# Twelve chained transformer stages on one core: the order of issue is planned with turns on the shared SBUF ports and with other durations for a few operations

## Chip, core and metric

The kernel runs on one core of a Trainium2 chip. The metric is the device time of one execution in microseconds (us). Engines are named as in the profile: PE (TensorE matmul), PEld (TensorE weight load), DVE (VectorE), ACT (ScalarE), POOL (GpSimd), SP (SyncE, which issues the DMAs).

## What is computed

One sequence of 512 tokens with 1024 features passes through two blocks of two layers each, in fp32. The first block has, per layer, a mixer of three parts (a chunked mLSTM, a chunked HGRN2 and a sliding window attention), an MLP with squared ReLU, and a gated embedding:

```
for l in range(2):
    h = rms_norm(x, in_norm_g[l]);  y = h @ w_in[l] + b_in[l]
    x = x + concat([mlstm(y), hgrn2(y), swa(y)]) @ w_out[l]
    x = x + square(relu(rms_norm(x, mlp_norm_g[l]) @ w_up[l])) @ w_down[l]
    x = x + sigmoid(rms_norm(x, ple_norm_g[l]) @ w_ple_gate[l]) * rms_norm(p[l] @ w_ple_proj[l], ...)
```

The second block has, per layer, self attention over all 512 tokens (layer 0 dilated, layer 1 differential), cross attention to 256 memory rows and a SwiGLU MLP, each followed by a normed residual addition.

## The kernel before

**Stages.** The program is a list of twelve stages, `b10, mlp0, ple0, b11, mlp1, ple1, attn0, cross0, ffn0, attn1, cross1, ffn1`. Activations lie feature-major: `x` is eight tiles of 128 features by 512 tokens. Every weight is streamed from HBM as a raw tile (`wr`, three buffers, 512 KB each in most cases). ACT rounds it to a high part (`wh`), DVE subtracts to get a low part (`wl = wr - wh`), and a product is three matmuls: high by high, low by high, high by low. Activations are split in the same way (`hi` on ACT, `lo` on DVE). The function `wload` does the first, `split` the second.

**Work outside the large products.** `hgrn_att` (four calls, two in each of b10 and b11) forms for nine level lengths a tile `X` (DVE subtracts, ACT takes the exponential, POOL multiplies by `key`) and a tile `B` (two POOL multiplies), then multiplies `X` by `B` on PE and selects the results into a tile `d` with six `copy_predicated` for each block of 128 columns. `hgrn_gates` holds the scans (`tensor_tensor_scan`, output `G`). `rope` is a DVE multiply, a DVE `stream_shuffle` and two POOL operations. `k_stacks` splits `kl` between DVE and POOL. `swa` and `score` take a row maximum together with the mask in one `tensor_tensor_reduce` (in the trace CUSTOM_DVE_ANT_0). The softmax scaling `P<-P,s` is in part a POOL multiply whose second operand is a column broadcast along the row. `stat_add` adds squares on POOL (`acc<-acc,sq`).

**What sets the order.** No instruction is issued as written. A `Recorder` collects every operation with its dependences (`add`), gives it a duration and a latency (`cost`, from line 409) and a mark `lock` if it needs the SBUF ports that DVE and POOL share (`locks`, from line 393: on POOL everything but `memset`, on DVE operations with two SBUF inputs, and `tensor_copy` and `tensor_scalar` from SBUF to SBUF). `schedule` (from line 467) then plays the program through in time, one list of ready operations for each engine, lowest priority number first. It models the ports as one lock: `lock` is the engine that holds it and when it ends. `emit` (line 644) issues the operations in the order that this plan found. The chip runs each engine's list in that order, whatever the planned times were; semaphores hold the dependences. So durations and port rules in the planner change nothing but the order, the buffers that go with it, and which engine does an operation that is marked `either` (the residual additions `x<-x,u` and `x<-x,y`, lines 1476 and 1586).

In the kernel before, an operation that finds the lock held by the other engine is taken off its list and comes back when the lock ends:

```python
if o.lock and lock[0] != e and lock[1] > now + 1e-9:
    seq += 1
    heapq.heappush(events, (lock[1], seq, e, ("ready", o)))
    continue
```

At that moment both engines are served in the fixed order tensor, vector, scalar, gpsimd, sync. A DVE operation that is ready and needs the lock therefore takes it ahead of a POOL operation that has been waiting, as often as DVE has another one.

In the trace nearly all instructions carry one line, L654, since `emit` issues them all. Groups are told apart by their tiles' names.

Of the kernel before, what the change touches and what calls it, by code (L numbers as in the profile page):

```python
# [283 lines left out]
DVE_FIX, DVE_EL, PTR_V = 67.0, 1.042, 61.0  # L284
# [13 lines left out]
class Recorder:  # L298
# [110 lines left out]
    def cost(self, o, outs, ins):  # L409
        n = int(np.prod(o.args[0].shape[1:])) if isinstance(o.args[0], View) else 512  # L410
        psum = any(v.tile.pool.space is not None for v in ins + outs)
        if o.eng == "tensor":
            k = (1 if o.fn != "transpose" and o.args[1].dtype == F32R and n >= 256 else 2 if o.fn == "transpose" else 4)
            o.cols = k * n * o.args[1].shape[0] / 128.0
            if o.fn == "transpose":
                return max(50.0, n / 1.2 + 1), 200.0
            if o.args[1].dtype == F32R:
                return (n / 2.4 + 13.3 if n >= 256 else 4 * n / 2.4 + 3), 200.0
            m = o.args[0].shape[0]
            least = 278.0 if m > 64 and n < 32 else 210.0 if m > 64 else 104.0 if m > 32 else 49.0  # L420
            d = max(least, 4 * (n / 2.4 + 1))
            if o.args[0].shape[0] == 64:
                o.cols /= 2
                o.half, o.work = outs[0].box()[0] // 64, d
            return d, 200.0
        ptr = sum(1 for v in list(o.args[2:]) + [v for k, v in o.kw.items() if k != "accum_out"]
                  if isinstance(v, View) and len(v.shape) == 2 and v.shape[-1] == 1)
        if o.eng == "scalar":
            acc = 93.0 if "accum_out" in o.kw else 0.0
            return (51.0 if (ins or outs)[0].tile.pool.space is not None else 93.0) + n * ACT_EL + PTR_A * ptr + acc, 130.0  # L430
        if o.eng == "vector":
            if o.fn == "reciprocal":
                return DVE_FIX + 8 * n, 130.0
            if o.fn in ("tensor_reduce",):
                n = int(np.prod((ins or outs)[0].shape[1:]))
            if o.fn == "tensor_tensor_reduce":
                return DVE_FIX + n * DVE_EL + 80, 130.0
            el = DVE_EL
            if o.fn in ("tensor_copy", "tensor_scalar") and not psum:
                el /= 2  # L440
            return DVE_FIX + n * el + (PTR_V * ptr if o.fn in ("tensor_scalar", "scalar_tensor_tensor") else 0), 130.0
        if o.eng == "gpsimd":
            if o.kw.get("op") == ALU.pow:
                return 300 + 165 * n, 150.0
            if o.fn == "memset":
                return 88.0, 150.0
            return 100 + 2.2 * n, 150.0
        rows = o.args[0].shape[0] if isinstance(o.args[0], View) else 128
        return 60.0 + rows * n * 4 / 330.0, 2000.0

# [16 lines left out]
    def schedule(self, window=6000):  # L467
# [24 lines left out]
        ready = {e: [] for e in ("tensor", "vector", "scalar", "gpsimd", "sync")}  # L492
# [7 lines left out]
        events = []  # L500
# [14 lines left out]
            return True  # L515

        nd = 0
        lock = None, 0.0
        table, self.loads = None, 0
        while nd < N:  # L520
            if not events:
# [21 lines left out]
            for e in ready:  # L543
                if free_at[e] > now + 1e-9:
                    continue
                q = ready[e]
                skipped = []
                pick = late = None
                while q:
                    pr, i = heapq.heappop(q)  # L550
                    o = ops[i]
                    if done[i]:
                        continue
                    if i > oldest + window:
                        skipped.append((pr, i))
                        if len(skipped) > SKIP:
                            break
                        continue
                    if not can(o) or (o.mate and not can(o.mate)):
                        skipped.append((pr, i))  # L560
                        if len(skipped) > SKIP:
                            break
                        continue
                    if e == "scalar" and now - o.ready < PATIENCE and o.table and table not in o.table:
                        skipped.append((pr, i))
                        late = late or o
                        continue
                    if e == "gpsimd" and o.alt:
                        wait = max(0.0, free_at["vector"] - now)
                        wait += sum(ops[n].dur for x, n in ready["vector"] if x < pr and not done[n])  # L570
                        if wait + o.dur <= o.alt[0]:
                            skipped.append((pr, i))
                            continue
                    at = max([t.held[1] + TURN for t in o.banks if t.held[0] != e], default=0.0)
                    if at > now + 1e-9:
                        seq += 1
                        heapq.heappush(events, (at, seq, e, ("ready", o)))
                        continue
                    if o.lock and lock[0] != e and lock[1] > now + 1e-9:
                        seq += 1  # L580
                        heapq.heappush(events, (lock[1], seq, e, ("ready", o)))
                        continue
                    pick = o
                    break
                if pick is None and late is not None:
                    pick = late
                    skipped.remove((late.prio, late.idx))
                for it in skipped:
                    heapq.heappush(q, it)
                if pick is None:  # L590
                    continue
                commit = [pick]
                if pick.mate is not None:
                    commit.append(pick.mate)
                if e == "gpsimd" and pick.alt:
                    pick.eng, (pick.dur, pick.lat) = "gpsimd", pick.alt
                for o in commit:
                    for t in o.tiles:
                        if not t.alloc:
                            t.alloc = True  # L600
                            k = (t.pool.name, t.tag)
                            used[k] += 1
                            if t.first > oldest:
                                prof[k][oldest:t.first] += 1
                    if e == "scalar" and o.table and table not in o.table:
                        table = o.table[0]
                        o.dur += TABLE_LOAD
                        self.loads += 1
                    if e == "tensor":
                        o.dur = self.clocked(now, o)  # L610
                    o.start, o.end = now, now + o.dur
                    if o.lock:
                        lock = e, o.end
                    for t in o.banks:
                        t.held = e, max(o.end, t.held[1])
                    order.append(o)
                    done[o.idx] = True
                    nd += 1
                while oldest < N and done[oldest]:
                    oldest += 1  # L620
                if len(commit) == 2:
                    o.start += PAIR
                    o.end += PAIR
                free_at[e] = o.end
                seq += 1
                heapq.heappush(events, (o.end, seq, e, None))
                for o in commit:
                    seq += 1
                    fin = o.end + (o.lat if e == "sync" else RELEASE)
                    heapq.heappush(events, (fin, seq, e, ("free", o)))  # L630
                    for u in o.users:
                        u.nleft -= 1
                        lat = SAME[e] if u.eng == e and e != "sync" and not u.alt else o.lat + (TO_PE if u.eng == "tensor" else 0.0)
                        u.ready = max(u.ready, o.end + lat)
                        m = u.mate
                        if u.nleft == 0 and (m is None or m.nleft == 0):
                            seq += 1
                            at = u.ready if m is None else max(u.ready, m.ready)
                            heapq.heappush(events, (max(at, now), seq, u.eng, ("ready", u)))
# [1325 lines left out]
```

## Time and profile before

| | |
|---|---|
| median of 3 runs (lowest to highest) | 3153.84 us (3153.36 to 3154.46) |
| profiled execution, own time | 3149.14 us |
| its span, first to last instruction | 3147.4 us |
| PE busy | 2988.2 us (95%) |
| DVE busy | 1888.0 us (60%) |
| ACT busy | 1421.3 us (45%) |
| POOL busy | 767.7 us (24%) |
| mean granted TensorE clock | 0.975 of full speed |

A row of a group gives the count, the busy time, the mean length of one instruction, and the idle time of its engine just before it with what ended that. A row of the timeline gives start, length, engine, operation, tiles written and read, and the count; the idle time before it stands in brackets. An instruction that waits for the shared ports shows as a longer instruction, not as idle time. DVE instructions that follow each other overlap by some 0.08 us in the records.

### The profile page before, as it was taken

How to read it: one execution, taken by the hardware profiler on the slowest of the kernel's cores; microseconds unless marked ns; L12 is line 12 of the kernel's file. 1: busy time of each engine (PE TensorE's matmuls, PEld its weight loads, DVE VectorE, ACT ScalarE, POOL GpSimd, SP SyncE). 2: the span in 40 equal slices, each digit the busy share in tenths (PEclk: the TensorE clock that was granted, in tenths of full speed). 3: DMA queues.
4: the chain of work that ended last, by engine and by line, in shares of the span. 5: the costliest groups of instructions: out<-in, count | busy, mean ns of one | idle time of the engine just before them, and what ended most of it. 6: DMA issues, size and time to landing. Idle time of an engine off the chain costs nothing. (4 is left out here: it accounts for less than half of the span.)

```text
span 3147.4 us, 42909 instructions
## 1 busy us (share of the span) xinstructions
PE 2988.2 (95%) x16480; PEld 2465.0 (78%) x16480; DVE 1888.0 (60%) x3429; ACT 1421.3 (45%) x2611; POOL 767.7 (24%) x619
## 2 busy tenths in 40 slices
PE   8879999999888999999999899999999998999998
PEld 6647888887656788888777787888897777998887
DVE  7667544458668644457767665433489876663434
ACT  7456433346365522244666544322356555542222
POOL 2554100031645200024544303000055532120001
PEclk9989999999889999999999999999999999999999
DMA  3201323222220322222112322232331213232323
GB/s 133 71 22 49 113 94 101 94 94 70 78 61 26 116 99 96 97 98 90 52 54 61 118 78 94 94 100 94 99 120 41 71 59 96 92 117 94 100 93 103
DMA packets 86613, 269.97 MB, mean 86 GB/s; under 512 B 9608, under 2 KB 12680, under 8 KB 86408
## 3 DMA queue, kind: packets, MB, share of 16 engines
q1 hardware_dynamic: 86408, 267.22, 26.4%
q8 instruction: 130, 2.13, 0.3%
q14 instruction: 75, 0.61, 0.1%
HBM read 265.09 MB, written 2.10 MB: 85 GB/s over the span
## 5 line engine op out<-in xcount | busy, mean ns | idle before, releaser
L654 ACT CAST wh<-wr 128x1024 fp32r<-128x1024 f32 (+2 forms) x482 | 483.2, 1006 | 1148.4 <-PE s L654 398.6
L654 DVE TENSOR_TENSOR wl<-wr,wh 128x1024 fp32r<-128x1024 f32 (+2 forms) x482 | 602.2, 1254 | 279.8 <-ACT wh L654 278.3
L654 PE MATMUL g<-hi,wh 128*128 128x512 f32 (+1 forms) x1756 | 679.0, 387 | 16.9 <-ACT hi L654 11.8
L654 PE MATMUL g<-hi,wl 128*128 128x512 f32 (+1 forms) x1756 | 676.6, 385 | 2.4 <-DVE wl L654 2.4
L654 PE MATMUL g<-lo,wh 128*128 128x512 f32 (+1 forms) x1756 | 677.6, 386 | 0.6 <-DVE lo L654 0.6
L654 PE MATMUL s<-lo,wh 128*128 128x512 f32 (+1 forms) x1732 | 652.7, 377 | 4.6 <-DVE lo L654 4.6
L654 PE MATMUL s<-hi,wh 128*128 128x512 f32 (+1 forms) x1732 | 652.7, 377 | 4.4 <-ACT hi L654 4.2
L654 PE MATMUL s<-hi,wl 128*128 128x512 f32 (+1 forms) x1732 | 652.3, 377 | 0.0
L654 PEld LDWEIGHTS g<-hi,wh 128*128 128x128 f32 x1756 | 334.6, 191 | 79.3 <-ACT hi L654 12.9
L654 PEld LDWEIGHTS g<-hi,wl 128*128 128x128 f32 x1756 | 334.7, 191 | 61.7 <-DVE wl L654 3.0
L654 PEld LDWEIGHTS g<-lo,wh 128*128 128x128 f32 x1756 | 334.2, 190 | 61.0 <-DVE lo L654 1.5
L654 POOL TENSOR_TENSOR acc<-acc,sq 128x512 f32<-128x512 f32 x101 | 156.4, 1549 | 915.4 <-ACT sq L654 902.7
L654 PEld LDWEIGHTS s<-lo,wh 128*128 128x128 f32 x1732 | 326.4, 189 | 65.1 <-DVE lo L654 7.9
L654 PEld LDWEIGHTS s<-hi,wh 128*128 128x128 f32 x1732 | 326.5, 188 | 63.6 <-ACT hi L654 5.9
L654 PEld LDWEIGHTS s<-hi,wl 128*128 128x128 f32 x1732 | 326.4, 189 | 57.2 <-issue 0.3
L654 POOL TENSOR_TENSOR sq<-sq,sq 128x512 f32<-128x512 f32 x24 | 38.0, 1585 | 741.8 <-ACT sq L654 741.5
L654 POOL TENSOR_TENSOR P<-P,s 128x512 f32<-128x512 f32 x96 | 111.3, 1168 | 145.0 <-DVE s L654 115.4
L654 POOL TENSOR_TENSOR s<-s,mhalf 128x4 f32<-128x4 f32 (+2 forms) x53 | 72.3, 1363 | 189.9 <-DVE s L654 189.5
L654 PE MATMUL t<-const,P 128*128 128x128 f32 x560 | 98.0, 283 | 13.4 <-ACT T L654 2.8
L654 DVE SCALAR_TENSOR_TENSOR lo<-x,cols,hi 128x512 fp32r<-128x512 f32 (+1 forms) x112 | 102.2, 934 | 5.2 <-ACT hi L654 5.0
L654 PEld LDWEIGHTS t<-const,P 128*128 128x128 f32 x560 | 64.7, 142 | 45.7 <-issue 25.9
L654 ACT ACTIVATE hi<-x,cols 128x512 fp32r<-128x512 f32 (+1 forms) x112 | 73.3, 658 | 59.1 <-DVE x L654 53.4
(308 smaller groups left out, 4497.9 us busy)
## 6 DMA issues: line engine op xcount, KB each, us to landing
wr<-in_w_down_dram SPq DMA_DIRECT2D x96, 512.0 KB, 3.3
wr<-in_gu_dram SPq DMA_DIRECT2D x88, 512.0 KB, 3.3
wr<-in_w_up_dram SPq DMA_DIRECT2D x64, 512.0 KB, 3.3
wr<-in_w_in_fm_dram SPq DMA_DIRECT2D x34, 512.0 KB, 3.4
wr<-in_qk_dram SPq DMA_DIRECT2D x32, 512.0 KB, 3.3
wr<-in_xo_dram SPq DMA_DIRECT2D x24, 512.0 KB, 3.4
wr<-in_w_down_dram SPq DMA_DIRECT2D x32, 384.0 KB, 3.1
wr<-in_w_out_dram SPq DMA_DIRECT2D x32, 256.0 KB, 2.7
```

What stands on the lines that cost most here:

```text
L654: getattr(getattr(nc, o.eng), o.fn)(*[res(a) for a in o.args], **{k: res(v) for k, v in o.kw.items()})
```

## The change

The planner is changed in two places; no operation is added or removed. In `cost`, a scan is given 45 + 2.09 ns an element, `copy_predicated` a fixed 213 ns, `stream_shuffle` 30 ns more than before, `tensor_tensor_reduce` loses 80 ns, and a POOL operation with a broadcast operand has 1.75 instead of 2.2 ns an element. In `schedule`, the engine that finds the lock held is noted in `claim`; its operation stays on the list. When the lock ends, an engine that is not the claimant passes over its lock operations until 15 ns after that, and takes another operation from its list or waits. A claim ends when the claimant issues anything.

```diff
-            if o.fn == "tensor_tensor_reduce":
-                return DVE_FIX + n * DVE_EL + 80, 130.0
+            if o.fn == "tensor_tensor_scan":
+                return 45.0 + 2.09 * n, 130.0
+            if o.fn == "copy_predicated":
+                return 213.0, 130.0
+            if o.fn == "stream_shuffle":
+                return DVE_FIX + n * DVE_EL + 30, 130.0
...
-            return 100 + 2.2 * n, 150.0
+            return 100 + (1.75 if any(0 in v.arr.strides for v in o.args if isinstance(v, View)) else 2.2) * n, 150.0
...
-        lock = None, 0.0
+        lock, claim = (None, 0.0), None
...
-                    if o.lock and lock[0] != e and lock[1] > now + 1e-9:
-                        seq += 1
-                        heapq.heappush(events, (lock[1], seq, e, ("ready", o)))
-                        continue
+                    if o.lock:
+                        if lock[1] > now + 1e-9:
+                            if lock[0] != e:
+                                claim = claim or e
+                                again = lock[1]
+                                skipped.append((pr, i))
+                                continue
+                        elif claim not in (None, e) and now < lock[1] + 15.0:
+                            again = lock[1] + 16.0
+                            skipped.append((pr, i))
+                            continue
...
                 if pick is None:
+                    if again is not None:
+                        seq += 1
+                        heapq.heappush(events, (again, seq, e, None))
                     continue
+                if claim == e or now > lock[1] + 15.0:
+                    claim = None
```

## Rows read from the trace of the kernel before

**Rows 1.** The page: span, and busy time of each engine.
```profile
span 3147.4 us, 42909 instructions
PE 2988.2 (95%) x16480; PEld 2465.0 (78%) x16480; DVE 1888.0 (60%) x3429; ACT 1421.3 (45%) x2611; POOL 767.7 (24%) x619
```

**Rows 2.** Windows of b10, b11, attn0, attn1: length; PE, PEld, DVE, ACT, POOL; clock; DMA.
```profile
0.00:310.00 310.00, 260.68 (x1715) 198.21 (x1716) 212.43 (x541) 175.31 (x411) 137.66 (x147) 0.90 0.21 66
...
755.00:1055.00 300.00, 253.21 (x1562) 189.30 (x1560) 230.41 (x539) 170.05 (x408) 143.97 (x124) 0.90 0.20 64
...
1470.00:1790.00 320.00, 304.54 (x1816) 242.47 (x1813) 225.02 (x480) 192.90 (x367) 150.85 (x105) 0.99 0.22 69
...
2290.00:2640.00 350.00, 322.94 (x2061) 275.90 (x2060) 294.11 (x614) 201.51 (x419) 174.99 (x124) 0.98 0.23 74
```

**Rows 3.** Groups of PE whose idle time POOL ended.
```profile
L654 PE MATMUL s<-B,X 128*64 128x64 f32 (+2 forms) x448 | 44.0, 296 | 31.8 <-POOL B L654 20.0 <-DVE d L654 5.3 <-ACT A L654 3.9
...
L654 PE MATMUL s<-qs,kl 128*128 128x256 f32 (+2 forms) x32 | 10.0, 366 | 10.3 <-POOL kl L654 10.3
```

**Rows 4.** Timeline of DVE and POOL at 315 us.
```profile
315.17 1.23 DVE L654 TENSOR_TENSOR wl<-wr,wh 128x1024 fp32r<-128x1024 f32 x1
316.31 1.78 DVE L654 SCALAR_TENSOR_TENSOR lo<-x,cols,hi 128x512 fp32r<-128x512 f32 x1
...
315.81 3.44 POOL L654 TENSOR_TENSOR acc<-acc,sq 128x512 f32<-128x512 f32 x2 [1.82 <-ACT sq L654]
```

**Rows 5.** Timeline of DVE and POOL at 788 us.
```profile
788.42 3.37 DVE L654 TENSOR_TENSOR wl<-wr,wh 128x1024 fp32r<-128x1024 f32 x3
...
787.97 5.12 POOL L654 TENSOR_TENSOR B<-X,qh 128x256 f32<-128x256 f32 x2 [0.94 <-DVE cr L654]
...
800.23 3.00 POOL L654 TENSOR_TENSOR B<-X,qh 128x256 f32<-128x256 f32 x4
```

**Rows 6.** Groups of DVE by shape that read two SBUF tensors: count, busy, mean.
```profile
L654 DVE TENSOR_TENSOR wl<-wr,wh 128x1024 fp32r<-128x1024 f32 x406 | 531.8, 1314 | 258.7 <-ACT wh L654 257.6
L654 DVE SCALAR_TENSOR_TENSOR lo<-x,cols,hi 128x512 fp32r<-128x512 f32 x80 | 80.6, 1029 | 4.8 <-ACT hi L654 4.6
...
L654 DVE TENSOR_TENSOR qs<-z,qs 64x512 fp32r<-64x512 f32 x48 | 43.9, 915 | 9.2 <-ACT qs L654 7.9
...
L654 DVE TENSOR_TENSOR kl<-z,kh 64x512 fp32r<-64x512 f32 x36 | 37.0, 1028 | 22.6 <-ACT kh L654 21.2 <-PE t L654 1.0
```

**Rows 7.** Single tiles: least/median/longest ns, first to last start.
```profile
L654 DVE TENSOR_TENSOR wl<-wr,wh x482: 667/1224/2353, 5.2 to 3127.4; 128x1024 fp32r<-128x1024 f32 x137, 128x512 fp32r<-128x512 f32 x10, 128x768 fp32r<-128x768 f32 x10, 128x972 fp32r<-128x972 f32 x2
...
L654 DVE SCALAR_TENSOR_TENSOR lo<-x,cols,hi x112: 468/746/1800, 9.2 to 2785.0; 128x512 fp32r<-128x512 f32 x80, 128x256 fp32r<-128x256 f32 x32
...
L654 DVE TENSOR_TENSOR qs<-z,qs x48: 684/687/1719, 234.1 to 2539.2; 64x512 fp32r<-64x512 f32 x48
...
L654 DVE TENSOR_TENSOR kl<-z,kh x36: 665/691/1780, 191.5 to 2544.1; 64x512 fp32r<-64x512 f32 x36
```

**Rows 8.** Operations whose planned duration changes: tiles, groups and a timeline row.
```profile
L654 POOL TENSOR_TENSOR P<-P,s x96: 1035/1042/1877, 257.3 to 2558.2; 128x512 f32<-128x512 f32 x96
...
L654 DVE TENSOR_TENSOR_SCAN G<-ls,zero 128x64 f32<-128x64 f32 x16 | 3.1, 268 | 0.0
...
L654 DVE COPY_PREDICATED d<-hm,s 128x64 f32<-128x64 int32 x96 | 23.0, 248 | 6.9 <-PE s L654 4.5
...
149.97 1.67 DVE L654 COPY_PREDICATED d<-hm,s 128x64 f32<-128x64 int32 x6 [1.46 <-PE s L654]
...
97.51 0.95 DVE L654 COPY_PREDICATED d<-hm,s 128x64 f32<-128x64 int32 x6
```

**Rows 9.** Timeline of DVE and POOL at 1501 us.
```profile
1501.33 0.19 DVE L654 TENSOR_SCALAR s<-s 128x1 f32<-128x1 f32 x2
...
1500.02 2.04 POOL L654 TENSOR_TENSOR P<-P,s 128x512 f32<-128x512 f32 x2 [0.99 <-DVE s L654]
```

**Rows 10.** Groups of DVE: small scalings of one column.
```profile
L654 DVE TENSOR_SCALAR s<-s 128x1 f32<-128x1 f32 x161 | 20.9, 143 | 0.3
```

More of the change, by code (lines that the diff above doesn't have):

```diff
@@ L547, in schedule @@
                 skipped = []
-                pick = late = None
+                pick = late = again = None
                 while q:
```

## The prediction

> **What bounds the kernel now.** I read the page first. PE is busy for 2988.2 of 3147.4 us [rows 1], so all that an order of issue can win lies in the 159.2 us in which PE is idle, and in what a low clock costs beside them. Next come the windows, cut at the stages [rows 2]. PE is idle for 310 - 260.7 = 49.3 us in b10, 300 - 253.2 = 46.8 in b11, 320 - 304.5 = 15.5 in attn0 and 350 - 322.9 = 27.1 in attn1: 138.7 us in 1280 us of span. The other eight stages share 20.5 us and can't be improved by an order. In these four DVE is busy for 69%, 77%, 70% and 84% of the time and POOL for 44% to 50%. These are the stages in which both engines are at work together, so they are where the ports matter. The clock was 0.90 of full speed in b10 and b11.
>
> Then I ask what ended PE's idle time. POOL ended 20.0 us of it ahead of the products of `X` and `B`, and 10.3 us ahead of the one that needs `kl` [rows 3]: 30.3 us, all in b10 and b11. DVE and ACT ended the rest in many small pieces.
>
> Last comes the ports' own price. An instruction that waits for them is longer in the trace. The mean against the median of the same operation gives the excess: `wl` (1314 - 1224) ns x 406 = 36.5 us, `lo<-x` (1029 - 746) x 80 = 22.6, `qs` (915 - 687) x 48 = 10.9, `kl` (1028 - 691) x 36 = 12.1 [rows 6, 7]. That is 82 us in which DVE stood still for POOL, and I found no other group of this size.
>
> **Does the chip take turns?** At 315 us it does [rows 4]. POOL asks at 315.81, while DVE's `wl` runs until 316.40. The next DVE instruction, a `lo`, starts at 316.31 and takes 1.78 us instead of 0.746: POOL went first, though DVE had its next instruction ready. The planner of before would have given DVE the ports again. So its plan holds POOL back too long and lets DVE run too smoothly, and the new plan is nearer to this row. At 788 us the chip does not take turns: two POOL multiplies take 5.12 us where four take 3.00 at 800 us, that is 3.6 us more, and meanwhile three `wl` pass in 3.37 us, undelayed [rows 5]. I take rows 4 as the common case: the medians of `qs` and `kl` are within 30 ns of their least values, and the longest are 1.03 and 1.1 us above them [rows 7], about one POOL operation (1.04 us in the median [rows 8]), which is what a DVE instruction pays that has lost one turn.
>
> **The change, part by part.**
>
> *The claim.* It adds no instruction and no wait on the chip; it moves instructions within the lists of DVE and POOL, and with them those of PE, ACT and SP (whose order of loads follows the weight buffers). It can win in two places. First, DVE. Where the plan now expects POOL to have its turn, it puts a DVE operation that needs no shared port (a move out of PSUM, for one) into that time, instead of a lock operation that on the chip would block the list behind it. What DVE loses, 82 us, reaches PE only where PE has nothing else: PE is idle for 138.7 / 1280 = 10.8% of these stages. Spread evenly, 82 x 0.108 = 8.9 us of it falls on PE. From both sides: nothing is won if no free operation is ready at those moments, all 8.9 if one always is. I take half, 4.5 us, since DVE is busy for some three quarters of the time and often has one. Second, POOL. The 30.3 us behind POOL are not removed, because POOL already gets its turns on the chip; what changes is that consumers are placed sooner after it, and its inputs ahead of other DVE work. Bounds: a loss of 10 us (one more stall like the one of `kl`) and a gain of 10 (one less). I take 5 us won, half of one such stall. Where a stall goes, the next thing late is DVE's `d` (5.3 us) and ACT's copies (3.9 us) on the same groups [rows 3], which is why I don't take more.
>
> *Scans.* The 64-column scan is recorded at 268 ns, and records overlap by some 80, so it holds DVE for about 188; the plan had 134, and has 179 now [rows 8]. The program has 66 scans; by the old and the new formula they gain 45 ns (64 columns) to some 500 ns (512 columns) each, all early in b10 and b11: about 7 us that the plan had not counted. On the chip nothing is shorter; I put the value at 0, between -2 and +2.
>
> *copy_predicated.* This one goes the wrong way. Six in a row take 1.67 us when each follows the last (289 ns a step) and 0.95 us when two chains interleave (about 145) [rows 8]. The plan had 134 plus 127 for the dependence, 261 a step, and now has 213 + 127 = 340. For 96 of them it believes that DVE is busy for 96 x 79 ns = 7.6 us more than before, in the stretches where `d` holds up PE. Worth 0, with -1 to +4 us: a slower plan of `d` puts PE's work behind it later.
>
> *Shuffle, mask and maximum, POOL with a broadcast.* 30 ns on 42 shuffles and 80 ns off 130 reductions move at most 1.3 and 10.4 us of planned DVE time, in stages where PE covers it. The POOL multiply is recorded at 1042 ns in the median; the plan had 1226 and has 996 [rows 8]. 96 of them, 22 us of planned POOL time, become available to the plan in swa, attn0 and attn1, which the chip had given already. All together 0, between -2 and +2.
>
> **The sum.** 4.5 + 5 = 9.5 us. The profiled execution took 3149.14 us, its span 3147.4 and 1.7 around it; it lies 4.7 us below the median of 3153.84. Its own time would become 3139.6, and the median 3153.8 - 9.5 = 3144.3, rounded to 3144.
>
> **Rivals.** *No difference.* The ports are given as in rows 5 often enough, or PE's idle time is set by chains (scan, exponential, multiply, product, select) that no order shortens. For it speaks that eight of twelve stages are PE work alone, and that POOL's turns come on the chip whatever the plan says. The time is 3153.8, give or take 6. The Trainium skill, in "SBUF — State Buffer", section "Who interferes with whom", says that whoever issues first has the shared pair for its whole instruction and the other blocks fully; it knows of no turn for the one who waits. By that rule the claim would describe nothing and this rival would hold; the 1.78 us of rows 4 speak against it, the 5.12 us of rows 5 for it.
>
> *Slower.* The planner marks the small column scalings `s<-s` as lock operations (161 of them). On the chip they don't wait: two take 0.19 us at 1501.33, in the midst of a POOL pair that runs from 1500.02 to 1502.06 [rows 9], and the mean over all is 143 ns [rows 10]. They stand between the row maximum and ACT's exponential in `score`, `cross` and `attn`. With a claim the plan passes over them at the end of a lock, waits for POOL's turn (1.04 us), and lets DVE take a longer operation of lower priority first (0.7 us, as `qs`). On the chip that is 0.7 us in front of a chain that PE waits for. It costs nothing where PE has other work; it decides if more than one in ten is moved onto a stretch where PE is idle: 16 x 0.7 = 11 us, so 3153.8 + 11 = 3165. DVE's 84% in attn1 makes that the place. Against it: these scalings come in bursts with other small ones, and priority brings them back at once.
>
> *The change hardly binds.* Any operation that the claimant issues ends its claim, so DVE's claims end at its next free operation. POOL has nothing but lock operations beside `memset`, so its claims hold; this rival is a part of the first.
>
> **How the numbers follow.** About 0.2%, 6.3 us, is what a measurement of this kernel can tell from no change. Forecast (a gain of more than that): 0.46. No difference: 0.30. Slower: 0.24. The forecast's own range is 3130 to 3147: both gains at their upper bounds give 8.9 + 10 = 19 us, and 2 to 5 more if the clock of 0.90 rises with less idle time. Reaching over the other cases, the range is 3128 to 3165, which leaves out a slower case beyond the price of one move in ten, and a gain beyond all bounds.
>
> **What would show it.** Right: PE's idle time falls by some 10 us in b10, b11 and attn1 together while PE's busy time stays; the means of `wl`, `lo` and `qs` fall towards their medians; POOL's share of PE's idle time falls below 25 us. Wrong on DVE: the excess of 82 us stays. Wrong on POOL: the waits for `B` or `kl` grow or new ones stand in their place. The slower rival: ACT's waits for `s` grow in attn1. The claim itself would be wrong if rows like 5 were found more often than rows like 4.

## The result, and the profile after

The changed kernel takes 3103.86 us (median of 4 runs, 3099.72 to 3105.31); the kernel before takes 3154.15 beside it. The ratio is 0.9838 with a 95% interval of 0.9821 to 0.9855: 50 us less, five times the forecast and outside its range. The profiled executions stand at 3105.31 and 3149.14 us, so the traces differ by 43.8 us, and what follows explains these. The other 6.5 us come from which execution was profiled: that of the kernel before is one of its faster ones, that of the changed kernel the slowest of its four.

The page of the changed kernel, span and busy time of each engine:

```profile
span 3103.5 us, 42865 instructions
PE 2983.3 (96%) x16480; PEld 2468.0 (80%) x16480; DVE 1859.7 (60%) x3407; ACT 1419.3 (46%) x2611; POOL 781.1 (25%) x641
```

Against [rows 1], PE is idle for 3103.5 - 2983.3 = 120.2 us instead of 159.2, that is 39.0 us less, and busy for 4.9 us less. DVE has 22 instructions fewer and POOL 22 more: so many residual additions `x<-x,y` have changed engine.

The windows of b10, b11, attn0 and attn1 in the changed kernel, columns as in [rows 2]:

```profile
0.00:296.00 296.00, 258.49 (x1713) 196.38 (x1714) 216.90 (x543) 176.16 (x413) 133.80 (x144) 0.93 0.23 73
740.00:1028.00 288.00, 248.73 (x1536) 190.07 (x1535) 221.54 (x534) 165.74 (x404) 146.06 (x129) 0.88 0.21 63
1443.00:1757.00 314.00, 305.98 (x1841) 243.61 (x1841) 212.58 (x471) 192.03 (x366) 152.88 (x110) 0.99 0.22 70
2251.00:2597.00 346.00, 326.21 (x2096) 279.41 (x2095) 281.95 (x606) 201.80 (x420) 179.85 (x134) 0.98 0.23 75
```

PE is idle there for 37.5, 39.3, 8.0 and 19.8 us, 104.6 in all instead of 138.7. So 34 of the 39 us were won in the four stages that the prediction named.

The groups of PE that answer to [rows 3], and two that POOL now holds up:

```profile
L670 PE MATMUL s<-B,X 128*64 128x64 f32 (+2 forms) x448 | 38.3, 278 | 20.3 <-POOL B L670 8.8 <-DVE d L670 7.2 <-ACT A L670 4.0
...
L670 PE MATMUL s<-qs,kl 128*128 128x256 f32 (+2 forms) x32 | 10.7, 389 | 0.3 <-POOL kl L670 0.3
...
L670 PE MATMUL t<-const,dn 128*64 128x1 f32 x96 | 5.1, 214 | 5.2 <-POOL dn L670 5.2
...
L670 PE MATMUL t<-const,qk 128*64 128x2 f32 x64 | 2.5, 200 | 3.2 <-POOL qk L670 3.2
```

In the two groups PE's waits for POOL fell from 30.3 us to 9.1, and 8.4 came back behind `dn` and `qk`: 12.8 us net. Summed over the whole trace by the engine that ended each idle stretch of PE, POOL went from 34.1 to 17.7 us, DVE from 80.6 to 57.1 and ACT from 35.4 to 36.5.

The groups of DVE that answer to [rows 6]:

```profile
L670 DVE TENSOR_TENSOR wl<-wr,wh 128x1024 fp32r<-128x1024 f32 x406 | 516.2, 1276 | 262.0 <-ACT wh L670 259.4 <-DMA kr<-in_xk_dram 1.7
...
L670 DVE SCALAR_TENSOR_TENSOR lo<-x,cols,hi 128x512 fp32r<-128x512 f32 x80 | 74.4, 950 | 4.0 <-ACT hi L670 3.4
...
L670 DVE TENSOR_TENSOR qs<-z,qs 64x512 fp32r<-64x512 f32 x48 | 44.4, 925 | 9.2 <-ACT qs L670 7.9
...
L670 DVE TENSOR_TENSOR kl<-z,kh 64x512 fp32r<-64x512 f32 x36 | 34.0, 944 | 7.0 <-ACT kh L670 6.3
```

By the working of the prediction, with the same medians, the excess is (1276 - 1224) x 406 + (950 - 746) x 80 + (925 - 687) x 48 + (944 - 691) x 36 = 57.9 us instead of 82: `wl` and `lo` lose fewer turns, `qs` none fewer. Two groups that the working leaves out went the other way: `lo<-x` with 256 columns from a mean of 697 to 900 ns (32 of them) and `X<-G` from 421 to 503 (48), 10 us more together.

**One stall, before and after.** The clearest place is in b10. The timeline of POOL, DVE and PE before, at 170 to 198 us:

```profile
169.86 1.76 POOL L654 TENSOR_TENSOR kl<-cv,kh 64x512 fp32r<-64x512 f32 x1 [2.14 <-PE s L654]
174.31 1.04 POOL L654 TENSOR_TENSOR C<-C 128x512 f32<-128x512 f32 x1 [2.69 <-ACT C L654]
177.05 1.64 POOL L654 TENSOR_TENSOR s<-s,mhalf 128x8 f32<-128x8 f32 x1 [1.71 <-DVE s L654]
182.60 1.64 POOL L654 TENSOR_TENSOR s<-s,mhalf 128x8 f32<-128x8 f32 x1 [3.92 <-DVE s L654]
188.23 1.26 POOL L654 TENSOR_TENSOR sh<-sh,S 128x512 f32<-128x512 f32 x1 [3.99 <-DVE sh L654]
189.57 1.26 POOL L654 TENSOR_TENSOR z<-z,sh 128x512 f32<-128x512 f32 x1
191.56 3.43 POOL L654 TENSOR_TENSOR kl<-z,kh 64x512 fp32r<-64x512 f32 x2 [0.73 <-ACT kh L654]
195.07 1.77 POOL L654 TENSOR_TENSOR kl<-cv,kh 64x512 fp32r<-64x512 f32 x1
...
195.02 0.69 DVE L654 TENSOR_TENSOR kl<-cv,kh 64x512 fp32r<-64x512 f32 x1 [1.16 <-POOL kl L654]
...
196.89 1.33 PE L654 MATMUL s<-qs,kl 128*128 128x512 f32 x3 [9.74 <-POOL kl L654]
```

and after, POOL at 152 to 164 us:

```profile
160.00 1.27 POOL L670 TENSOR_TENSOR kl<-cv,kh 64x512 fp32r<-64x512 f32 x1 [9.13 <-ACT A L670]
161.87 1.28 POOL L670 TENSOR_TENSOR kl<-cv,kh 64x512 fp32r<-64x512 f32 x1 [0.59 <-ACT A L670]
```

Before, seven operations of the window attention (norm, rope and key split) stand between the first and the second `kl` of the mLSTM on POOL's list. POOL is idle for 13.0 us among them, waiting for their inputs, though ACT had finished the second `kl`'s own input by 169.2 us; PE waits 9.74 us for it. After, both `kl` come one behind the other, the second 33 us earlier, and that wait of PE is gone. What changed here is the order on POOL's own list. That the ports alone put it there is not shown. DVE's half of the same tile, on another list, comes as late (195.02), and what ends DVE's wait is POOL's `kl<-z,kh`, whose result it does not read. That looks like a wait for a buffer, and the plan agrees: played through, the planner of before passes over both halves from 155 to 181 us of its own time because none of the 58 buffers for activations (`NT`) can be given out; at two moments DVE's half could have had one, and POOL held the ports.

**Where along the program.** The DMA that fetches the last `w_ple_gate` tile marks the end of the first block's work, the first `gu` tile the end of cross0, and the last `w_down` tile the end of the program. The rows of these tiles (least/median/longest ns of the issue, first to last start), kernel before:

```profile
L654 SPq DMA_DIRECT2D wr<-in_w_ple_gate_dram x16: 327/328/328, 651.3 to 1418.1; - x16
L654 SPq DMA_DIRECT2D wr<-in_gu_dram x88: 327/328/328, 1892.2 to 3057.1; - x88
L654 SPq DMA_DIRECT2D wr<-in_w_down_dram x128: 327/328/328, 335.2 to 3117.5; - x128
```

changed kernel:

```profile
L670 SPq DMA_DIRECT2D wr<-in_w_ple_gate_dram x16: 327/328/328, 635.8 to 1391.5; - x16
L670 SPq DMA_DIRECT2D wr<-in_gu_dram x88: 327/328/328, 1856.7 to 3013.3; - x88
L670 SPq DMA_DIRECT2D wr<-in_w_down_dram x128: 327/328/328, 319.6 to 3073.4; - x128
```

Three stretches follow: A from the start to the last `w_ple_gate` (b10 to ple1), 1418.1 us before and 1391.5 after (-26.6); B from there to the first `gu` (attn0, cross0), 474.1 and 465.2 (-8.9); C to the last `w_down` (ffn0, attn1, cross1, ffn1), 1225.3 and 1216.7 (-8.6). In A the gain lies in b10 and b11: their windows above are 14 and 12 us shorter than in [rows 2].

### The profile page after: what moved, and what is told of

It reads as the page before. It is cut to its first block, busy times and chain, and to the rows that moved or that the text cites. A ratio compares the mean times of both kernels' runs of the same rounds, so it can differ in the third digit from the quotient of the medians.

```text
span 3103.5 us, 42865 instructions
## 1 busy us (share of the span) xinstructions
PE 2983.3 (96%) x16480; PEld 2468.0 (80%) x16480; DVE 1859.7 (60%) x3407; ACT 1419.3 (46%) x2611; POOL 781.1 (25%) x641
## 3 DMA queue, kind: packets, MB, share of 16 engines
q1 hardware_dynamic: 86408, 267.22, 26.6%
## 4 chain that ended last, share of the span: by engine, by line
PE 84%; DVE 7%; ACT 3%; POOL 3%; issue 1%; DMA 1%; POOLq 0%; SPq 0%; DVEq 0%; ACTq 0%
PE s L670 44%; PE g L670 37%; PE t L670 4%; DVE y L670 1%; POOL B L670 1%; DVE wl L670 1%; ACT kh L670 1%; DVE s L670 1%; DVE kl L670 1%; DVE lo L670 1%; DVE G L670 0%; DVE P L670 0%; ACT P L670 0%; ACT W L670 0%; DMA kr<-in_xv_dram 0%
## 5 line engine op out<-in xcount | busy, mean ns | idle before, releaser
L670 DVE TENSOR_TENSOR wl<-wr,wh 128x1024 fp32r<-128x1024 f32 (+2 forms) x482 | 585.4, 1219 | 290.9 <-ACT wh L670 287.9
L670 POOL TENSOR_TENSOR acc<-acc,sq 128x512 f32<-128x512 f32 x101 | 150.0, 1485 | 922.3 <-ACT sq L670 906.8
L670 POOL TENSOR_TENSOR sh<-sh,S 128x512 f32<-128x512 f32 x42 | 68.2, 1623 | 105.4 <-DVE sh L670 51.3
```

The costliest lines, as they stand in the source:

```text
L670: getattr(getattr(nc, o.eng), o.fn)(*[res(a) for a in o.args], **{k: res(v) for k, v in o.kw.items()})
```

## The experiments

Fifteen kernels ran, each a variant of the planner alone. All times are medians; the last three columns are the stretches of the profiled execution, formed from the same three rows of each trace. The ratio is to the kernel before as it ran beside each variant; its medians there lay between 3151.4 and 3154.1 us.

| kernel | claim | five durations | else | us | ratio to before (95%) | A | B | C |
|---|---|---|---|---|---|---|---|---|
| before | | | | 3154 | | 1418.1 | 474.1 | 1225.3 |
| changed | yes | yes | | 3103.9 | 0.9838 (0.9821 to 0.9855) | 1391.5 | 465.2 | 1216.7 |
| claim_only | yes | | | 3097.7 | 0.9827 (0.9809 to 0.9845) | 1379.4 | 461.9 | 1224.5 |
| keep_only | | | list kept | 3154.3 | 1.0002 (0.9991 to 1.0013) | 1421.3 | 474.4 | 1229.8 |
| dur_only | | yes | | 3162.2 | 1.0027 (1.0016 to 1.0038) | 1410.7 | 478.0 | 1240.9 |
| nudge_before | | | DVE + 1 ns | 3146.6 | 0.9984 (0.9974 to 0.9993) | 1412.0 | 470.0 | 1231.9 |
| nudge_claim | yes | | DVE + 1 ns | 3096.6 | 0.9830 (0.9813 to 0.9846) | 1379.2 | 463.9 | 1222.1 |
| nudge_after | yes | yes | DVE + 1 ns | 3115.4 | 0.9879 (0.9864 to 0.9894) | 1395.8 | 463.2 | 1223.7 |
| no_ports | | | no lock in the plan | 3174.3 | 1.0079 (1.0064 to 1.0094) | 1384.0 | 505.6 | 1254.7 |
| pool_first | | | POOL served first | 3147.3 | 0.9987 (0.9978 to 0.9996) | 1390.9 | 478.8 | 1247.1 |
| claim_early | A, start of B | | | 3110.1 | 0.9862 (0.9847 to 0.9877) | 1380.0 | 473.4 | 1223.9 |
| old_pred | yes | four of five | | 3101.7 | 0.9848 (0.9833 to 0.9862) | 1379.9 | 464.0 | 1228.2 |
| true_pool | yes | | POOL from rows | 3098.6 | 0.9823 (0.9808 to 0.9838) | 1382.9 | 464.1 | 1220.5 |
| small_free_alone | | | small ops free | 3153.9 | 1.0000 (0.9991 to 1.0010) | 1412.7 | 469.7 | 1235.5 |
| small_free_claim | yes | | small ops free | 3084.8 | 0.9784 (0.9768 to 0.9800) | 1376.9 | 460.4 | 1214.9 |
| small_free_nudge | yes | | small ops free, + 1 ns | 3098.8 | 0.9828 (0.9813 to 0.9842) | 1377.9 | 463.1 | 1226.1 |
| small_free_after | yes | yes | small ops free | 3087.1 | 0.9790 (0.9775 to 0.9804) | 1370.9 | 465.0 | 1217.3 |

### Which half of the change does it

claim_only is the changed kernel with `cost` as before:

```diff
-            if o.fn == "tensor_tensor_scan":
-                return 45.0 + 2.09 * n, 130.0
-            if o.fn == "copy_predicated":
-                return 213.0, 130.0
-            if o.fn == "stream_shuffle":
-                return DVE_FIX + n * DVE_EL + 30, 130.0
+            if o.fn == "tensor_tensor_reduce":
+                return DVE_FIX + n * DVE_EL + 80, 130.0
...
-            return 100 + (1.75 if any(0 in v.arr.strides for v in o.args if isinstance(v, View)) else 2.2) * n, 150.0
+            return 100 + 2.2 * n, 150.0
```

> The changed schedule, with all planned durations as before. Turns theory (the order gained because the plan now gives POOL its turn as the chip does): at least 35 of the 50 us, so 3119 us or less. Durations theory (the gain comes from the mended durations): within 10 us of 3154. Luck theory (any shift of the plan moves the time by tens of us): anywhere from 3090 to 3180, with no sum over the parts.

Measured 3097.7 us: the claim alone brings 56 us, more than the whole change. PE's idle time is as low as in the changed kernel, 3095.9 - 2975.3 = 120.6 us:

```profile
span 3095.9 us, 42892 instructions
PE 2975.3 (96%) x16480; PEld 2463.7 (80%) x16480; DVE 1872.8 (60%) x3407; ACT 1422.4 (46%) x2611; POOL 789.8 (26%) x641
```

dur_only is the reverse: the kernel before with these lines of `cost` as in the changed kernel, and its own `schedule`.

```diff
-            return 100 + 2.2 * n, 150.0
+            return 100 + (1.75 if any(0 in v.arr.strides for v in o.args if isinstance(v, View)) else 2.2) * n, 150.0
...
```

> The five new durations with the schedule of before. Turns theory: between 3139 and 3160. Durations theory: 3119 or less. Luck theory: anywhere from 3090 to 3180.

Measured 3162.2, 8 us above, and 2 above the range of the turns theory. The durations don't carry the gain.

keep_only keeps the new loop, with the durations of before, and takes the claim out:

```diff
-                                claim = claim or e
```

> Durations as before, and the new loop without the claim: an operation that finds the ports held stays on its list instead of leaving it until the lock ends. The one effect that I see is that DVE's list looks longer when the planner chooses the engine of a residual addition, so that more of them go to POOL (43 instead of 21 in the changed kernel). Turns theory: within 8 us of 3154. Engine-choice theory (the gain is that 22 additions left DVE): 20 us or more below 3154.

Measured 3154.3. Its lists of instructions turned out to be those of before, one for one, on all engines: my reason for more additions on POOL was wrong, since the shift to POOL comes from the claim. So it is a repeat of the kernel before, and tells what a repeat is worth: the median within 1 us, and up to 5 us between the stretches of two profiled executions.

It therefore doesn't test the engine-choice theory. Two kernels below do. The engines' lines of their pages, claim_early, then pool_first:

```profile
PE 2977.0 (96%) x16480; PEld 2464.0 (79%) x16480; DVE 1880.7 (61%) x3429; ACT 1421.1 (46%) x2611; POOL 766.8 (25%) x619
```

```profile
PE 2991.1 (95%) x16480; PEld 2471.7 (79%) x16480; DVE 1843.2 (59%) x3405; ACT 1422.0 (45%) x2611; POOL 758.0 (24%) x643
```

claim_early moves no addition (x3429 and x619, as before) and has nearly the claim's whole gain in A. pool_first moves 24 and is longer than before in B and C. So the moved additions explain nothing in A, and alone they bring nothing in B; that they help there beside the claim is not excluded.

nudge_before asks how much an order changes by luck:

```diff
-DVE_FIX, DVE_EL, PTR_V = 67.0, 1.042, 61.0
+DVE_FIX, DVE_EL, PTR_V = 68.0, 1.042, 61.0
```

> The kernel before with the fixed part of every planned DVE duration at 68 instead of 67 ns, which is as true as the other value. Turns and durations theories: within 8 us of 3154. Luck theory: 10 us or more away from it, on either side.

Measured 3146.6: one nanosecond in the plan, 7.5 us on the chip by the medians, 2 to 8 by the interval of the ratio. nudge_claim is the same line on claim_only, and nudge_after on the changed kernel:

> The claim with the durations of before, and the fixed part of every planned DVE duration at 68 instead of 67 ns. If the claim's gain is a property of its rule: within 12 us of 3098, as the same nudge moved the kernel before by 7.5 us. If it is the luck of one order: back to 3125 or more.

> The changed kernel with the fixed part of every planned DVE duration at 68 instead of 67 ns. If the five durations truly cost 6 us beside the claim: 3104 within 4. If those 6 us are the luck of an order, as large as the 7.5 us that this nudge moved the kernel before: anywhere from 3090 to 3112.

Measured 3096.6, as its first case has it, and 3115.4, above both ranges. The claim's gain outlives the nudge: with and without the claim, else alike, there are four pairs, 3097.7 against 3154, 3096.6 against 3146.6, 3103.9 against 3162.2, and (below) 3084.8 against 3153.9. That is 50 to 69 us each. Single differences of some 12 us, on the other hand, are within what a nudge does, and I read none of them alone as an effect below.

The same four pairs show what the gain is made of. PE's idle time is the span less PE's busy time, from the page of each run; the clock is the mean granted one of that execution, as a share of the full 2.4 GHz. A mean below 1 is time at the lower level, 1.2 GHz, most of it in b10 and b11 ([rows 2]: 0.90 there, 0.98 and 0.99 in attn1 and attn0).

| pair, without and with the claim | PE idle, us | PE busy, us | clock |
|---|---|---|---|
| before, claim_only | 159.2, 120.6 (-38.6) | 2988.2, 2975.3 (-12.9) | 0.975, 0.977 |
| nudge_before, nudge_claim | 159.4, 118.4 (-41.0) | 2985.0, 2976.6 (-8.4) | 0.977, 0.978 |
| dur_only, changed | 159.9, 120.2 (-39.7) | 3000.2, 2983.3 (-16.9) | 0.970, 0.976 |
| small_free_alone, small_free_claim | 147.2, 112.3 (-34.9) | 3000.6, 2969.8 (-30.8) | 0.972, 0.982 |
| keep_only, the repeat of before | 156.6 | 2998.8 | 0.970 |

The idle time that the claim takes away is nearly the same in each pair, 35 to 41 us. The rest is the same matmuls at another clock: busy time multiplied by clock is 2907 to 2917 us in every row. One order alone moves by 10.6 us in this way (before and its repeat). The 7.5 us of nudge_before are of this kind too, since its idle time is that of before.

### Is it turns as on the chip, or only POOL earlier?

The claim does two things to the plan: POOL is no longer held back behind runs of DVE work, and DVE loses time to POOL as in rows 4. no_ports does the first without the second, in the kernel before:

```diff
-        o.lock = self.locks(o)
+        o.lock = False
```

> The kernel before, with a plan that knows of no shared ports: neither DVE nor POOL ever waits for the other in it. Durations as before. Fidelity theory (the gain needs a plan in which both wait as on the chip): 3140 us or more, since DVE is planned without the time it loses. Early-POOL theory (the gain is only that the plan no longer holds POOL back behind runs of DVE work): 3120 us or less, like the claim.

Measured 3174.3, slower than before by some 23 us beside it. The stretches show that this is a gain and a larger loss. The three rows of no_ports:

```profile
L654 SPq DMA_DIRECT2D wr<-in_w_ple_gate_dram x16: 327/328/328, 634.0 to 1384.0; - x16
L654 SPq DMA_DIRECT2D wr<-in_gu_dram x88: 327/328/328, 1889.6 to 3084.0; - x88
L654 SPq DMA_DIRECT2D wr<-in_w_down_dram x128: 327/328/328, 316.6 to 3144.3; - x128
```

In A it is 34.1 us faster than before, nearly the claim's 38.7. In B it is 31.5 us slower, in C 29.4. So in b10 and b11 it is nearly enough that the plan doesn't hold POOL back; in the attention stages a plan without ports costs time. What goes wrong there can be read from PE's waits in B (sum in us, times, longest), first the largest three in no_ports, 1384 to 1889.6 us:

```profile
PE s L654 <- DVE kl L654: 12.2, 7, 3.5
PE s L654 <- ACT kh L654: 8.6, 6, 1.9
PE g L654 <- DVE lo L654: 3.0, 2, 2.7
```

then in claim_only (1379.4 to 1841.3 us, all that it lists there):

```profile
PE s L666 <- DVE kl L666: 2.8, 1, 2.8
PE g L666 <- DVE kl L666: 1.7, 2, 1.2
PE t L666 <- POOL acc L666: 0.2, 1, 0.2
```

PE's products into `s` wait for `kh` and `kl` (the split keys of the attention, whose `kl` DVE and POOL share, and weights of cross attention under the same names): 20.8 us where the claim's plan has 2.8. The windows of B, columns as in [rows 2], no_ports, then claim_only:

```profile
1384.00:1889.60 505.60, 471.86 (x2765) 383.56 (x2765) 324.45 (x663) 267.00 (x506) 165.18 (x118) 0.97 0.21 70
```

```profile
1379.40:1841.30 461.90, 456.99 (x2763) 375.52 (x2762) 308.85 (x663) 266.64 (x507) 171.99 (x120) 0.99 0.24 77
```

PE is idle for 33.7 us instead of 4.9, so these waits are 18 of the 28.8 us more; and it is busy for 14.9 us more with the same work, at a granted clock of 0.97 of full speed instead of 0.99. DVE is busy for 15.6 us more with as many instructions: that is time of the kind that this plan doesn't count.

pool_first is the mirror of the old fault. The kernel before, with POOL served ahead of DVE at the end of a lock:

```diff
-            for e in ready:
+            for e in ("tensor", "gpsimd", "vector", "scalar", "sync"):
```

> The kernel before, with POOL served ahead of DVE when both want the ports at the same moment, so that the plan holds DVE back behind runs of POOL work: the mirror of the fault of before. Durations as before. Fidelity theory: above the claim's 3098 by 20 us or more, so 3118 or more. Early-POOL theory: 3105 us or less.

Measured 3147.3: A gains 27.2 us, B loses 4.7 and C 21.8. Early POOL alone is again good for b10 and b11 and bad for the rest. By the whole time the fidelity theory holds; in A early POOL alone brings most of the gain.

claim_early lets only the first 9957 of the planner's operations claim. attn0 starts at 9596, so that is the first block and the first eighth of attn0:

```diff
-                                claim = claim or e
+                                claim = claim or (e if i < 9957 else None)
```

> The claim alone, durations as before, but only for operations of the first block (b10 to ple1); in the second block nobody claims. If each stage has its own gain: the first block 39 us sooner, as with the claim throughout, and little more after it, so 3108 to 3122. If the second block's gain came from what the first hands on (which stage starts with which buffers): near 3098.

Measured 3110.1. A gains 38.1 us, B and C 0.7 and 1.4, less than a repeat is worth: a stretch keeps its gain, and nothing of it is seen to be handed on. The rows:

```profile
L666 SPq DMA_DIRECT2D wr<-in_w_ple_gate_dram x16: 327/328/328, 636.1 to 1380.0; - x16
L666 SPq DMA_DIRECT2D wr<-in_gu_dram x88: 327/328/328, 1853.4 to 3017.0; - x88
L666 SPq DMA_DIRECT2D wr<-in_w_down_dram x128: 327/328/328, 321.7 to 3077.3; - x128
```

Of the 51.7 us by which the three stretches of claim_only are shorter than those of before, 38.7 thus belong to A and 12.2 to B.

### The durations, and small operations

old_pred is the changed kernel without its line for `copy_predicated`:

```diff
-            if o.fn == "copy_predicated":
-                return 213.0, 130.0
```

> The changed kernel with copy_predicated planned as before (134 instead of 213 ns), all else as changed. If that term is the part that goes the wrong way: 2 to 6 us below the changed kernel's 3104, above all in b11, where the changed kernel lost 11 us against the claim alone. If the difference of 6 us between them is the luck of an order: within 8 us of 3104 on either side, with no sign of b11.

Measured 3101.7, 2.2 us below the changed kernel, with executions that overlap its own (3098.41 to 3103.76 against 3099.72 to 3105.31). A is 11.6 us shorter, C 11.5 longer. It fits the forecast's sign, and doesn't show it.

true_pool gives the claim POOL durations from the undisturbed rows:

```diff
-            return 100 + 2.2 * n, 150.0
+            return 175 + 2.18 * n, 150.0
```

> The claim alone, with POOL's planned durations set by the undisturbed rows: 175 + 2.18 ns an element, so 733 ns for 256 columns (trace 735) and 1291 for 512 (trace 1290), instead of 663 and 1226. Fidelity theory: 3 to 12 us below the claim's 3098, in b10 and b11 above all, where POOL multiplies 256 columns. If an order is only as good as its luck: 3090 to 3108 with no sign of those stages.

Measured 3098.6, no change, where its fidelity theory had 3 to 12 us less. Five to eleven per cent on POOL's durations matter less than who gets the ports.

small_free_claim is claim_only with small copies and scalings taken out of the planned lock, since [rows 9, 10] show that those of one column don't wait. The edit goes up to 16 columns, further than these rows: one `s<-s` of 8 columns took 1254 ns where the median of the four is 172:

```diff
         if o.fn in ("tensor_copy", "tensor_scalar"):
+            if o.args[0].shape[-1] <= 16:
+                return False
```

> The claim alone, durations as before, and tensor_copy and tensor_scalar of at most 16 columns no longer planned as users of the ports. My slower rival named these as what the claim would mis-plan. If that costs anything: 3 to 12 us below 3098, above all in attn0, cross and attn1, where they stand in front of the exponential. If not: within 8 us of 3098.

Measured 3084.8: 13 us below the claim alone, 19 us below the changed kernel, and the fastest of all. Three more runs ask whether that is a rule.

> The claim, no ports for small copies and scalings, and the fixed part of every planned DVE duration at 68 instead of 67 ns. If the 13 us that the small operations brought are a property of the rule: 3091 or less. If they are the luck of an order: within 8 us of the claim's 3098 or above.

> The kernel before with no ports for small copies and scalings, without the claim. If that mend is worth something by itself: 3140 to 3147. If it matters only where POOL has claims (my slower rival's mechanism, in which a claim pushes these operations back): within 6 us of 3153.

> The changed kernel (claim and the five durations) with no ports for small copies and scalings. A fourth pair with and without the durations, beside 3162 and 3154, 3104 and 3098, 3115 and 3097. If the five durations together are a loss by themselves: 3089 or more against 3085. If their sign is the luck of each order: at or below 3085 in about one pair of two.

Measured 3098.8, 3153.9 and 3087.1. Against their partners without the line: -12.8 (claim_only), +2.2 (nudge_claim), -0.1 (before), -16.8 (changed). Without the claim it does nothing; with it, two pairs gain and one doesn't, all within or just beyond what a nudge does. By its own forecast 3098.8 is the case of luck, and 3087.1 falls between the two cases of its own. Whether the line is worth 10 us or the orders were lucky stays open. The five durations have four pairs, too: +8 (dur_only), +6 (changed against claim_only), +19 (nudge_after against nudge_claim), +2 (small_free_after against small_free_claim). All of one sign, so a small loss is likely; none alone shows it. Against claim_only the changed kernel's PE is idle just as long (120.2 and 120.6 us); its loss is busy time.

## Why the prediction was right in its sign and wrong in its size

- **The direction held, and so did the places.** The plan that gives turns is the better one, and 34 of the 39 us of idle time went from the four stages named. What failed is the size, at three terms.
- **The term for POOL, 5 us with a bound of 10, measured 12.8 net in the groups named (21.2 gone, 8.4 new) and 16.4 over the whole trace.** The step said that "POOL already gets its turns on the chip" and that only consumers move. That was the error: POOL's own list changes, as the `kl` of b10 shows. Why the old plan had that one so late is open; buffers and ports both had a part. Rows 3 held 30.3 us, and the bound should have been all of it.
- **The term for DVE, 4.5 us with a bound of 8.9, measured 23.5: PE's waits for DVE, 80.6 us before and 57.1 after.** The step that failed is "Spread evenly": it let DVE's 82 us reach PE at the rate of PE's idle share, 10.8%. In the changed kernel the excess of the four groups fell by 24 us and PE's waits for DVE by as much, but this is no rule of one for one. In claim_only they fell by 16.5 and 13.9 us. In pool_first the excess fell to 53.9 us and PE's waits for DVE to 62.7, and PE's idle time by 3.7 us only, since its waits for ACT grew from 35.4 to 53.3. So the price cannot be read from DVE's lost time alone; how a lost turn reaches PE stays open. The bound that needs no such assumption was the 138.7 us of PE's idle time in the four stages, less the 9.1 us before PE's first instruction.
- **The clock was left out of the sum and given 2 to 5 us in the range.** PE's busy time fell by 4.9 us between the two profiled executions, but by 8 to 31 in the four pairs. The four executions of claim_only had a mean clock of 0.977, those of before beside it 0.9725; with 2910 us of busy time at full clock that is some 14 us, an estimate from these rows. Idle time and clock, 39 and 14, come to 53 of the claim's 56 us.
- **How far luck enters.** A nudge moved single orders by up to 14 us, so part of the 50 may be the luck of this order. The claim's 50 to 69 us in four pairs are more than that.
- **Terms put at 0.** Scans, shuffle, reductions and the broadcast, together with `copy_predicated`: +2 to +19 us in four pairs, so 0 was too kind and the upper ends (2, 4 and 2) too near. That the step for `copy_predicated` goes the wrong way fits old_pred by 2.2 us, and isn't shown.
- **The rivals.** "No difference" fell: a plan that gives turns is worth 50 us and more. The Trainium skill's rule in "SBUF — State Buffer", section "Who interferes with whom", is that whoever issues first keeps the pair while the other blocks. The `lo` of rows 4, 1.78 us instead of 0.746, agrees. The rule says nothing of who is next, and it matters here whom the plan lets go next: 3097.7 us with a claim, 3154 with DVE always first and 3147.3 with POOL first. The slower rival did not come: ACT's waits for the row maximum went from 67.0 to 56.6 us, in attn1 from 19.6 to 16.8. Its premise, that the small scalings are mis-planned, may still be worth 10 us on the other side, see above.

## What to carry to other kernels

If a static order is made by playing the program through, the rule for a shared resource can be worth more than better durations: here who gets the ports next was worth 50 to 69 us, and five durations taken from rows nothing or a small loss. Bound such a change by all the idle time that the waits for the two engines end, not by a share of it, and where the idle time lies in stretches of a low clock, count the clock as a term of its own. And before a few us are read as an effect, shift the plan by a meaningless nanosecond: here that alone moved the time by up to 14 us.

## What the runs showed that I had not expected

POOL still loses several turns in a row on the chip now and then, in the changed kernel too. POOL and DVE there at 67 us:

```profile
66.91 6.92 POOL L670 TENSOR_TENSOR qk<-y,key 128x512 f32<-128x512 f32 x1 [4.27 <-DVE y L670]
...
67.82 0.47 DVE L670 TENSOR_SCALAR qh<-y,const 128x512 f32<-128x512 f32 x1
68.21 1.08 DVE L670 TENSOR_TENSOR X<-G 128x256 f32<-128x256 f32 x3
...
69.28 3.42 DVE L670 TENSOR_TENSOR wl<-wr,wh 128x1024 fp32r<-128x1024 f32 x3
```

A multiply that takes 1.31 us in the mean before (its four took 5.3 us) takes 6.92, while at least seven DVE instructions pass undelayed. PE then waits 3.2 us for `qk`. Rows 4 and this one show two behaviours of the same ports; what tells them apart was not tried. The first is the common one, as the prediction took it. In the trace of before, 95 of the 1038 instructions of DVE that write `wl`, `lo`, `qs`, `kl` or `X` take over 0.6 us more than the shortest of their kind, and in only eight instructions of POOL do two or more of them pass undelayed; in the changed kernel it is 71 and three.
